# Modulation vectors of a two-layer trunk: formed by TensorE in four column groups, zero rows written by the fillers

## The chip, the core and the metric

One core of a Trainium2 chip runs the whole program in one launch. The metric is the device time of one execution in microseconds, the median of several. The engines of the core work in parallel, each through its own instruction queue in order: TensorE (matrix products, PE in the profile, its weight loads PEld), VectorE (DVE), ScalarE (ACT), GpSimd (POOL), and SyncE (SP), which issues most of the DMAs. Sixteen DMA engines carry the transfers. All tensors are float32.

## The reference

Two layers over 512 latent and 256 context tokens of 1024 channels. Each layer draws its modulation from two condition vectors:

```
s_lat, s_ctx = silu(c), silu(c_ctx)
sh1, sc1, g1, sh2, sc2, g2 = split(s_lat @ w_mod[layer] + b_mod[layer], 6)   # the same for s_ctx
h = rmsnorm(x, norm1_g) * (1 + sc1) + sh1
y = token_mixer(h)        # w_in, a short gated convolution beside RWKV-7 scans in both directions, gates, w_o
x = x + g1 * y
h2 = rmsnorm(x, norm2_g) * (1 + sc2) + sh2
x = x + g2 * hier_moe(h2) # the top expert group of 4, then the top 2 of its 8 SwiGLU experts
```

In the last layer the context feeds only the scans' first states. A final norm gives the output. The modulation is a product of two vectors of 1024 with a matrix of 1024 x 6144, per layer: 24 MB of weights that are read once.

## The kernel before

The 6144 modulation columns of a layer are worked off as twelve groups g of 512. Groups 0 and 1 are the shift sh1, 2 and 3 the scale sc1, 4 and 5 the gate g1, and so on. A group's weights are eight tiles of 128x512, one for each 128 inputs. The inputs, silu of both conditions, lie in `sc` (128 x 8 x 2).

The stages of a layer follow one another: a start-up (layer 0 only, `startup`), the dense stage (`stage_dense`, 15 products with w_in and what the scans need), the scans (`stage_scan`), the output products (`stage_out`), the 32 experts (`moe`, whose weights are 192 MB a layer), and `combine`. The scans are two passes of 12 chunks each, a chain of small products per chunk with copies by ScalarE and VectorE between them. Ahead of each six chunks `inverses` inverts triangular blocks by 31 steps of a multiply (line 834) and an add (line 836) on VectorE; TensorE takes them up at line 858.

Between the links of that chain TensorE is given other work, from a generator, `fillers` (line 638): the remaining products with w_in, the convolution, the gates, and w_a_out. It is advanced one `yield` at a time; a step is the products of one 128-channel tile of a filler (six in layer 0, three in layer 1). 12 and 18 steps are taken in the dense stage, the rest in the scans, 0.75 steps for each unit of weight that the chain's links state. TensorE's order is the written one in the dense stage and the scans (`manual_schedule`); that of VectorE, ScalarE, GpSimd and SyncE is the planner's, which may put an instruction well ahead of its place in the program once its inputs and buffers are there. In the start-up SyncE's order is the written one too.

The modulation vectors are made in two ways.

- Start-up, groups 0 to 3 of layer 0, `modulate` (line 251): two loads of 1 MB, eight products of the two columns of `sc` with 128x512 into one accumulator of two rows; ScalarE copies the two rows out (line 267), and four products turn them into columns (line 270).
- Everything else, 12 groups in the fillers of layer 0 (the last four are layer 1's) and 8 in those of layer 1, `mod_begin` and `mod_end` (lines 225 and 244), called by `more` (line 651) at 13 places of a layer's fillers. `mod_begin` loads eight tiles of 256 KB, ScalarE multiplies each by one column of `sc` for each condition that is needed (lines 237 and 240), and GpSimd adds it to an accumulator (line 241). The next `more` calls `mod_end`: four products with ones for each condition sum over the partitions (line 249), and `mod_store` adds the bias and derives what follows from it.

The experts' outputs go to `bufY` in HBM. Its part for overflowing experts, 24 x 64 rows (6.3 MB), is written with zeros in the start-up by `zero_rows` (line 160): three DMAs of 2 MB out of a tile of 128 zeros, in rows of 512 bytes.

PSUM buffers come by tag. `pd` has three, shared by the fillers' outputs (two in layer 0, one in layer 1), the final sums and, in the start-up, the accumulator.

Of the kernel before, what the change touches and what calls it, by code (L numbers as in the profile page):

```python
# [18 lines left out]
P = 128  # L19
D = 1024  # L20
KT = 8
# [46 lines left out]
for _n, _w in (("ident", 128), ("mask", 128), ("bones", 128), ("bmean", 128), ("ones", 128), ("ii", 64), ("tri", 128),  # L68
               ("i64", 64), ("i8", 8), ("i4", 4), ("i24", 24), ("i64k", 12), ("tok", 6)):
    CO[_n] = slice(_o, _o + _w)  # L70
    _o += _w
# [3 lines left out]
def constants():  # L75
    c = np.zeros((P, NCO), np.float32)
    p = np.arange(P)[:, None]
    q = np.arange(P)[None, :]
    c[:, CO["ident"]] = p == q
    s = p % C  # L80
    t = q % C
    c[:, CO["mask"]] = np.where(q < C, s < t, s <= t)
    c[:, CO["bones"]] = (p // 64) == (q // 64)
    c[:, CO["bmean"]] = ((p // 64) == (q // 64)) * (-1.0 / 64)
    c[:, CO["ones"]] = 1.0
    c[:, CO["ii"]] = (p % 64) == np.arange(64)[None, :]
    c[:, CO["tri"]] = p < q
    c[:, CO["i64"]] = np.arange(64)
    c[:, CO["tok"]] = p + P * np.arange(6)
    c[:, CO["i8"]] = np.arange(8)  # L90
    c[:, CO["i4"]] = np.arange(4)
    c[:, CO["i24"]] = np.arange(24)
    c[:, CO["i64k"]] = 64.0 * (1 + np.arange(12))
    m = np.zeros((P, T + 1024), np.float32)
    m[:, :T] = (np.arange(T) % C) != 0
    m[:, T:] = np.eye(32, dtype=np.float32).reshape(1, 1024)
    return c, m
# [16 lines left out]
class Trunk:  # L114
# [12 lines left out]
    def build(self):  # L127
        nc, tc, t = self.nc, self.tc, self.t
        with ExitStack() as es:
# [3 lines left out]
            sc = self.sc = self.sb(cp, [P, KT, 2], "sc")  # L133
# [11 lines left out]
            nc.vector.tensor_scalar(sc, th, 0.5, None, op0=ALU.mult)  # L145
# [14 lines left out]
    def zero_rows(self, pool):  # L160
# [6 lines left out]
        for i in range(0, n, 4096):  # L167
            nc.sync.dma_start(v[:, i:i + 4096].rearrange("p (a d) -> p a d", d=128),
                              rap(z[:], 0, [[0, 32], [1, 128]]))
# [55 lines left out]
    def mod_begin(self, l, g, pool, bufs):  # L225


        nc, t = self.nc, self.t
        ns = 2 if l == 0 or g < 4 else 1
        acc = [self.sb(pool, [P, 512], f"ma{s}") for s in range(ns)]  # L230
        for k in range(KT):
            w = self.sb(pool, [P, 512], "wm", bufs=bufs)
            nc.sync.dma_start(w, t["w_mod"][l, g][:, k, :])
            for s in reversed(range(ns)):
                c = self.sc[:, k, s:s + 1]
                if k == 0:
                    nc.scalar.activation(acc[s], w, AF.Copy, scale=c)  # L237
                else:
                    p = self.sb(pool, [P, 512], "wms") if s else w
                    nc.scalar.activation(p, w, AF.Copy, scale=c)  # L240
                    nc.gpsimd.tensor_tensor(acc[s], acc[s], p, op=ALU.add)  # L241
        return l, g, ns, acc

    def mod_end(self, l, g, ns, acc):

        ps = self.psum("pd", [P, 4, 2], bufs=3)
        for m in range(4):
            for s in range(ns):
                self.nc.tensor.matmul(ps[:, m, s:s + 1], acc[s][:, m * P:(m + 1) * P], self.k["ones"][:, :1],
                                      start=True, stop=True)  # L250
        self.mod_store(l, g, ns, ps)

    def modulate(self, l, g, pool, loads=()):

        nc, k = self.nc, self.k
        ps = self.psum("pd", [2, 512], 3)
        for h in range(2):
            w = self.sb(pool, [P, 4, 512], "wm", bufs=6)
            nc.sync.dma_start(w, self.t["w_mod"][l, g][:, 4 * h:4 * h + 4, :])
            for i in range(4):  # L260
                kt = 4 * h + i
                nc.tensor.matmul(ps, self.sc[:, kt, :], w[:, i, :], start=kt == 0, stop=kt == KT - 1)
            yield
        for src, dst in loads:
            nc.sync.dma_start(dst, src)
        row = self.sb(pool, [2, 512], "mrow", bufs=2)
        nc.scalar.activation(row, ps, AF.Copy)
        ps = self.psum("pc", [P, 4, 2], 2)
        for m in range(4):
            nc.tensor.matmul(ps[:, m, :], row[:, m * P:(m + 1) * P], k["ident"][:2, :2], start=True, stop=True)  # L270
        self.mod_store(l, g, 2, ps)
# [97 lines left out]
    def startup(self):  # L369

        nc, tc, k, V = self.nc, self.tc, self.k, self.nc.vector
        with tc.tile_pool(name="np", bufs=1, side=self.B, reuse_waits="tile") as np_:
# [20 lines left out]
            with tc.high_priority(offset=10000), tc.manual_schedule(engines=MAN(E)):  # L393
# [29 lines left out]
                self.zero_rows(np_)  # L423
# [215 lines left out]
    def fillers(self, fp, mods):  # L639
# [8 lines left out]
        mods = iter(mods)  # L648
        begun = []

        def more():
            if begun:
                self.mod_end(*begun.pop())
            g = next(mods, None)
            if g is not None:
                begun.append(self.mod_begin(*g, fp, 3))
        cw = pv[:, PV["cw"]].rearrange("p (w j) -> p w j", j=4)
        for j in range(4):
# [6 lines left out]
            groups = []  # L665
            for ps, s in (yield from self.w_in_parts(i0 + 1)):
# [16 lines left out]
        for m in range(16):  # L683
# [4 lines left out]
            if m % 2:  # L688
                more()
# [3 lines left out]
        for m in range(8):  # L693
            if m == 2:
# [858 lines left out]
```

## Time and profile before

| | |
|---|---|
| median of 3 runs | 3068.42 us (3065.1 to 3070.13) |
| profiled execution | 3077.6 us, its span 3075.6 us |
| PE | 2592.5 us (84%), 17281 instructions |
| PEld | 1718.6 us (56%) |
| DVE | 1332.2 us (43%), 2597 |
| ACT | 995.0 us (32%), 1839 |
| POOL | 716.2 us (23%), 778 |
| HBM | 647.41 MB read, 91.49 MB written, 240 GB/s over the span |
| mean granted TensorE clock | 0.909 of full speed |

Busy times are sums over the whole span; a share says how full an engine is, not whether anything waits for it. A float32 product stands in the trace as two records with a weight load each. The idle time given with an instruction is that of its engine just before it, and the name behind the arrow is what ended it. The granted clock is a mean over a stretch of the two levels, 1.2 and 2.4 GHz, in parts of the upper one.

### The profile page before, as it was taken

How to read it: one execution, taken by the hardware profiler on the slowest of the kernel's cores; microseconds unless marked ns; L12 is line 12 of the kernel's file. 1: busy time of each engine (PE TensorE's matmuls, PEld its weight loads, DVE VectorE, ACT ScalarE, POOL GpSimd, SP SyncE). 2: the span in 40 equal slices, each digit the busy share in tenths (PEclk: the TensorE clock that was granted, in tenths of full speed). 3: DMA queues.
4: the chain of work that ended last, by engine and by line, in shares of the span. 5: the costliest groups of instructions: out<-in, count | busy, mean ns of one | idle time of the engine just before them, and what ended most of it. 6: DMA issues, size and time to landing. Idle time of an engine off the chain costs nothing. (4 is left out here: it accounts for less than half of the span.)

```text
span 3075.6 us, 44626 instructions
## 1 busy us (share of the span) xinstructions
PE 2592.5 (84%) x17281; PEld 1718.6 (56%) x17281; DVE 1332.2 (43%) x2597; ACT 995.0 (32%) x1839; POOL 716.2 (23%) x778
## 2 busy tenths in 40 slices
PE   7998688798889699977887996788888969888886
PEld 4777576676778643333336775566666734333334
DVE  4786564656345421111115687556565431111113
ACT  4653445454512111111112553443442211111111
POOL 0431344544521100000002232233222021000001
PEclk9999898889889899999997998778899979999998
DMA  8456344443546699999994466444534599999994
GB/s 301 131 160 193 105 123 139 147 158 121 163 153 214 227 344 402 398 402 396 401 360 153 134 184 209 133 141 153 157 121 149 194 337 398 395 399 394 399 400 161
DMA packets 301974, 741.87 MB, mean 241 GB/s; under 512 B 55488, under 2 KB 140736, under 8 KB 250816
## 3 DMA queue, kind: packets, MB, share of 16 engines
q1 hardware_dynamic: 288480, 694.42, 62.7%
q0 software_dynamic: 13280, 44.57, 4.4%
q8 instruction: 137, 2.24, 0.3%
q14 instruction: 77, 0.63, 0.1%
HBM read 647.41 MB, written 91.49 MB: 240 GB/s over the span
## 5 line engine op out<-in xcount | busy, mean ns | idle before, releaser
L341 PE MATMUL pd<-hh,wh 128*128 128x512 f32 (+1 forms) x912 | 362.5, 437 | 11.1 <-DVE fo L1490 3.4
L341 PE MATMUL pd<-hh,wl 128*128 128x512 f32 (+1 forms) x912 | 318.9, 391 | 11.0 <-DVE wl L323 11.0
L341 PE MATMUL pd<-hl,wh 128*128 128x512 f32 (+1 forms) x912 | 318.4, 390 | 0.6 <-DVE hl L323 0.6
L323 DVE TENSOR_TENSOR wl<-wr,wh 128x512 fp32r<-128x512 f32 x236 | 183.5, 779 | 258.5 <-ACT wh L322 257.1
L1393 PE MATMUL pd<-ez,xs 128*64 128x512 f32 x1024 | 253.9, 630 | 39.3 <-DMA ez<-in_w 25.1
L1402 DVE COPY hs<-pd 128x512 f32<-128x512 f32 x65 | 45.0, 692 | 521.4 <-PE pd L1393 521.4
L322 ACT ACTIVATE wh<-wr 128x512 fp32r<-128x512 f32 x236 | 148.2, 629 | 295.7 <-PE pd L341 198.9
L241 POOL TENSOR_TENSOR ma<-ma,wm 128x512 f32<-128x512 f32 x140 | 187.2, 1337 | 164.5 <-ACT ma L237 118.2
L341 PEld LDWEIGHTS pd<-hh,wh 128*128 128x128 f32 x912 | 169.2, 204 | 59.2 <-issue 13.6
L1369 POOL DMA_INDIRECT xe<-h2rows,slot x64 | 60.0, 937 | 592.5 <-PE px L1381 552.8
L341 PEld LDWEIGHTS pd<-hh,wl 128*128 128x128 f32 x912 | 169.0, 204 | 48.8 <-DVE wl L323 15.0
L1414 DVE TENSOR_TENSOR yo<-py,yo 64x1024 f32<-64x1024 f32 x65 | 79.1, 1216 | 263.6 <-ACT yo L1413 252.3
L1406 PEld LDWEIGHTS pt<-cst,hs 128*128 128x128 f32 x1040 | 125.1, 191 | 112.7 <-issue 54.3
L341 PEld LDWEIGHTS pd<-hl,wh 128*128 128x128 f32 x912 | 170.3, 206 | 29.3 <-issue 1.9
L1393 PE MATMUL pd<-er,xs 128*64 128x512 f32 x672 | 169.4, 624 | 18.9 <-DMA er<-in_w 9.8
L1393 PEld LDWEIGHTS pd<-ez,xs 128*64 128x64 f32 x1024 | 78.0, 143 | 174.4 <-issue 126.6
L1406 PE MATMUL pt<-cst,hs 128*128 128x64 f32 x1040 | 141.3, 281 | 27.6 <-DVE hs L1402 17.4
L1393 PE MATMUL py<-ez,hid 128*64 128x512 f32 x520 | 123.3, 605 | 11.7 <-DVE yo L1414 7.4
L1415 POOL DMA_DIRECT2D bufY<-yo x65 | 35.5, 547 | 418.7 <-DVE yo L1414 391.7
L1408 ACT ACTIVATE hid<-pt 128x256 f32<-128x256 f32 x65 | 24.9, 383 | 321.4 <-PE pt L1406 320.7
L1383 ACT ACTIVATE xs<-px 128x512 f32<-128x512 f32 x65 | 38.8, 597 | 272.2 <-PE px L1381 263.1
L241 POOL TENSOR_TENSOR ma<-ma,wms 128x512 f32<-128x512 f32 x84 | 111.2, 1323 | 58.7 <-ACT wms L240 58.0
(379 smaller groups left out, 4977.8 us busy)
## 6 DMA issues: line engine op xcount, KB each, us to landing
ez<-in_w SPq DMA_DIRECT2D x193, 1024.0 KB, 22.6
er<-in_w SPq DMA_DIRECT2D x125, 1024.0 KB, 22.6
ex<-in_w SPq DMA_DIRECT2D x72, 1024.0 KB, 22.5
wr<-in_w_in SPq DMA_DIRECT2D x172, 256.0 KB, 3.1
wm<-in_w_mod SPq DMA_DIRECT2D x160, 256.0 KB, 3.5
bufY<-yo POOLq DMA_DIRECT2D x65, 256.0 KB
dKB<-KB SPq DMA_DIRECT2D x16, 768.0 KB, 4.5
dRR<-RR SPq DMA_DIRECT2D x16, 768.0 KB, 5.1
```

The source lines that it names most:

```text
L241: nc.gpsimd.tensor_tensor(acc[s], acc[s], p, op=ALU.add)
L322: self.nc.scalar.activation(hi, src, AF.Copy)
L323: self.nc.vector.tensor_tensor(lo, src, hi, op=ALU.subtract)
L341: nc.tensor.matmul(p, a[:, k], h[:, kt, s], start=kt == 0 and j == 0, stop=kt == nk - 1 and j == 2)
L1369: self.nc.gpsimd.indirect_dma_start(out=xe[:], out_offset=None, in_=self.h2[:], in_offset=bass.IndirectOffsetOnAxis(ap=slot, axis=0))
L1383: nc.scalar.activation(xs, ps, AF.Copy)
L1393: nc.tensor.matmul(out[h * CAP:(h + 1) * CAP, c:c + 512], a[:, kt, :], w[:, i + h, c:c + 512], start=kt < 2, stop=kt >= nk - 2)
L1402: nc.vector.tensor_copy(hs, ps)
L1406: nc.tensor.matmul(pt[:, i, c, :], hs[:, c * P:(c + 1) * P], k["ii"], start=True, stop=True)
L1408: nc.scalar.activation(hid, pt[:, 0], AF.Silu)
L1414: nc.vector.tensor_tensor(yo, py[:CAP], yo, op=ALU.add)
L1415: nc.gpsimd.dma_start(ydst, yo)
```

## The change

`sc` becomes 128 x 8 x 32, with zeros behind its two columns, so that a product with it fills 32 rows of PSUM. Product kt of a group goes to the rows from 32 x (kt mod 4): four column groups of the array, each with its own rows of one accumulator. ScalarE copies all 128 rows out; four products with a new constant `sel` (128 x 2, ones where the partition modulo 32 is 0 or 1) add the four column groups up and turn them into columns at once.

In the start-up two products fall on each column group and accumulate there. In the fillers a group comes in two halves of four tiles, one load of 1 MB each into a single buffer, four products that don't accumulate; the first half is copied to `row` by ScalarE, the second added to it by VectorE. `more` now does three things: the final sums of a finished group, the products of the half loaded at the call before, and the load of the next half. It is called twice as often. ScalarE's scalings and GpSimd's additions are gone; the products form both vectors for every group, of which the groups of layer 1 that need one store one.

`zero_rows` becomes a generator that writes 512 KB at a time, and in layer 0 each `more` advances it once: twelve DMAs from the fillers instead of three in the start-up.

```diff
-            sc = self.sc = self.sb(cp, [P, KT, 2], "sc")
+            sc = self.sc = self.sb(cp, [P, KT, 32], "sc")
...
+            nc.vector.memset(sc, 0.0)
+            nc.vector.tensor_scalar(sc[:, :, :2], th, 0.5, None, op0=ALU.mult)
...
+    c[:, CO["sel"]] = (p % 32) == np.arange(2)[None, :]
...
-        for i in range(0, n, 4096):
-            nc.sync.dma_start(v[:, i:i + 4096].rearrange("p (a d) -> p a d", d=128),
-                              rap(z[:], 0, [[0, 32], [1, 128]]))
+        for i in range(0, n, 1024):
+            nc.sync.dma_start(v[:, i:i + 1024].rearrange("p (a d) -> p a d", d=128),
+                              rap(z[:], 0, [[0, 8], [1, 128]]))
+            yield
...
-    def mod_begin(self, l, g, pool, bufs):
...
-    def mod_end(self, l, g, ns, acc):
...
+    def mod_load(self, l, g, h, n, pool, bufs):
+        w = self.sb(pool, [P, n, 512], "wm", bufs=bufs)
+        self.nc.sync.dma_start(w, self.t["w_mod"][l, g][:, h:h + n, :])
+        return w
+    def mod_products(self, ps, w, h, n):
+        for i in range(n):
+            kt = h + i
+            self.nc.tensor.matmul(ps[32 * (kt % 4):32 * (kt % 4) + 32, :], self.sc[:, kt, :], w[:, i, :],
+                                  start=kt < 4, stop=kt >= KT - 4)
+    def mod_rows(self, ps, pool, bufs):
+        row = self.sb(pool, [P, 512], "mrow", bufs=bufs)
+        self.nc.scalar.activation(row, ps, AF.Copy)
+        return row
+    def mod_sums(self, l, g, ns, row, tag, bufs):
+        ps = self.psum(tag, [P, 4, 2], bufs)
         for m in range(4):
+            self.nc.tensor.matmul(ps[:, m, :], row[:, m * P:(m + 1) * P], self.k["sel"], start=True, stop=True)
         self.mod_store(l, g, ns, ps)
     def modulate(self, l, g, pool, loads=()):
...
+        ps = self.psum("pd", bufs=3)
+        for h in (0, 4):
+            self.mod_products(ps, self.mod_load(l, g, h, 4, pool, 6), h, 4)
             yield
         for src, dst in loads:
+            self.nc.sync.dma_start(dst, src)
+        self.mod_sums(l, g, 2, self.mod_rows(ps, pool, 2), "pc", 2)
...
                 advance(self.modulate(0, 3, np_))
-                self.zero_rows(np_)
                 shifted(range(4, 8))
...
+        mods = ((i, h) for i in mods for h in (0, 4))
+        loaded, rows, done = [], [], []
+        zeros = self.zero_rows(fp) if l == 0 else iter(())
         def more():
+            if done:
+                i = done.pop()
+                self.mod_sums(*i, 2 if i[0] == 0 or i[1] < 4 else 1, rows.pop(), "pd", 3)
+            if loaded:
+                i, h, w = loaded.pop()
+                ps = self.psum("pd", bufs=3)
+                for kt in range(4):
+                    nc.tensor.matmul(ps[32 * kt:32 * kt + 32, :], self.sc[:, h + kt, :], w[:, kt, :],
+                                     start=True, stop=True)
+                if h:
+                    nc.vector.tensor_tensor(rows[0], rows[0], ps, op=ALU.add)
+                    done.append(i)
+                else:
+                    rows.append(self.mod_rows(ps, fp, 1))
+            i, h = next(mods, (None, 0))
+            if i is not None:
+                loaded.append((i, h, self.mod_load(*i, h, 4, fp, 1)))
+            next(zeros, None)
...
             groups = []
+            more()
...
+            more()
             for ps, s in (yield from self.w_in_parts(i0 + 2)):
...
-            if m % 2:
-                more()
+            more()
...
-            if m == 2:
+            if m in (2, 4):
                 more()
```

## Rows read from the trace of the kernel before

**Rows 1.** Windows by stage: length, busy time (instructions) by engine, granted clock, DMA share, GB/s

```profile
300.00:345.00 45.00, 20.83 (x188) 17.85 (x187) 38.00 (x61) 18.14 (x27) 20.88 (x16) 0.73 0.27 81
345.00:890.00 545.00, 473.79 (x4463) 389.55 (x4458) 289.23 (x617) 262.53 (x522) 246.60 (x253) 0.90 0.44 140
...
1090.00:1610.00 520.00, 447.15 (x2276) 190.73 (x2278) 80.37 (x116) 81.32 (x125) 43.38 (x60) 0.96 1.00 394
...
1940.00:2380.00 440.00, 376.19 (x3604) 284.37 (x3599) 241.93 (x541) 179.24 (x382) 129.15 (x170) 0.87 0.47 148
```

**Rows 2.** Costliest groups: GpSimd's additions (count, busy us, mean ns, idle before)

```profile
L241 POOL TENSOR_TENSOR ma<-ma,wm 128x512 f32<-128x512 f32 x140 | 187.2, 1337 | 164.5 <-ACT ma L237 118.2
...
L241 POOL TENSOR_TENSOR ma<-ma,wms 128x512 f32<-128x512 f32 x84 | 111.2, 1323 | 58.7 <-ACT wms L240 58.0
```

**Rows 3.** Timeline, first inverse of layer 0 (start, duration, operation, [idle before])

```profile
308.03 0.42 DVE L834 TENSOR_TENSOR tmp<-AlTc,Tl 128x252 f32<-128x252 f32 x1
...
314.49 1.38 DVE L834 TENSOR_TENSOR tmp<-AlTc,Tl 128x252 f32<-128x252 f32 x1
...
329.18 1.30 DVE L834 TENSOR_TENSOR tmp<-AlTc,Tl 128x192 f32<-128x192 f32 x1
...
338.93 1.49 PE L858 MATMUL pA<-AlTc,AM 32*32 32x32 f32 x48 [23.75 <-DVE AlTc L840]
```

**Rows 4.** Timeline, first inverse of layer 1

```profile
1905.01 1.37 DVE L834 TENSOR_TENSOR tmp<-AlTc,Tl 128x192 f32<-128x192 f32 x1
...
1917.21 1.36 DVE L836 TENSOR_TENSOR Tl<-Tl,tmp 128x252 f32<-128x252 f32 x1
...
1935.42 1.49 PE L858 MATMUL pA<-AlTc,AM 32*32 32x32 f32 x48 [27.08 <-DVE AlTc L840]
```

**Rows 5.** Timeline, a readout in the scan of layer 0

```profile
606.79 5.39 DVE L834 TENSOR_TENSOR tmp<-AlTc,Tl 128x252 f32<-128x252 f32 x1
...
615.04 1.20 PE L1004 MATMUL pA<-cst,yr 128*128 128x128 f32 x4 [9.07 <-DVE yr L312]
```

**Rows 6.** TensorE's groups in 340 to 890, the idle time before them

```profile
L952 PE MATMUL pc<-VU,KTr 128*64 128x64 f32 x352 | 17.4, 240 | 10.9 <-DVE VU L944 10.7
...
L1004 PE MATMUL pA<-cst,yr 128*128 128x128 f32 x44 | 9.1, 337 | 22.4 <-DVE yr L312 20.7 <-DVE AM L817 1.7
```

**Rows 7.** The same in 1940 to 2380

```profile
L943 PE MATMUL pc<-W,Rf 64*64 64x64 f32 x384 | 18.1, 240 | 23.0 <-ACT W L936 23.0
...
L1004 PE MATMUL pA<-cst,yr 128*128 128x128 f32 x32 | 7.1, 356 | 9.5 <-DVE yr L312 8.9 <-DVE AM L817 0.6
```

**Rows 8.** ScalarE's scalings in 1950 to 2370

```profile
L240 ACT ACTIVATE wm<-wm,sc 128x512 f32<-128x512 f32 x40 | 28.6, 719 | 41.2 <-DMA wm<-in_w_mod 40.1 <-POOL ma L241 0.8
```

**Rows 9.** Timeline of the start-up, TensorE, SyncE and ScalarE

```profile
6.80 8.47 PE L262 MATMUL pd<-wm,sc 128*2 128x512 f32 x16 [6.80 <-DMA wm<-in_w_mod]
...
23.80 22.23 SPq L168 DMA_DIRECT2D bufY<-zrow  x3
...
35.67 7.03 PE L262 MATMUL pd<-wm,sc 128*2 128x512 f32 x16
...
38.92 2.50 ACT L390 ACTIVATE nh<-xin,mod,am 128x512 f32<-128x512 f32 x4 [4.28 <-DVE mod L276]
...
61.32 0.50 PE L341 MATMUL pd<-hh,wh 128*128 128x512 f32 x1 [1.39 <-ACT hh L322]
```

**Rows 10.** Timeline of an expert: products that alternate between two column groups

```profile
1206.98 3.65 PE L1393 MATMUL pd<-ez,xs 128*64 128x512 f32 x16 [0.69 <-ACT xs L1383]
```

**Rows 11.** Timeline: final sums of two vectors and of one

```profile
310.11 1.84 PE L249 MATMUL pd<-cst,ma 128*128 128x1 f32 x16
...
1903.09 0.95 PE L249 MATMUL pd<-cst,ma 128*128 128x1 f32 x8
```

**Rows 12.** Timeline: the two pairs behind 64-row products

```profile
277.10 0.63 PE L341 MATMUL pd<-hh,wh 128*128 128x512 f32 x2
277.56 0.51 PE L341 MATMUL pd<-hl,wh 128*128 128x512 f32 x2
```

More of the change, by code (lines that the diff above doesn't have):

```diff
@@ L68 @@
 for _n, _w in (("ident", 128), ("mask", 128), ("bones", 128), ("bmean", 128), ("ones", 128), ("ii", 64), ("tri", 128),
-               ("i64", 64), ("i8", 8), ("i4", 4), ("i24", 24), ("i64k", 12), ("tok", 6)):
+               ("i64", 64), ("sel", 2), ("i8", 8), ("i4", 4), ("i24", 24), ("i64k", 12), ("tok", 6)):
     CO[_n] = slice(_o, _o + _w)
@@ L144, in build @@
             nc.vector.scalar_tensor_tensor(th, th, 1.0, cv, op0=ALU.add, op1=ALU.mult)
-            nc.vector.tensor_scalar(sc, th, 0.5, None, op0=ALU.mult)
+            nc.vector.memset(sc, 0.0)
+            nc.vector.tensor_scalar(sc[:, :, :2], th, 0.5, None, op0=ALU.mult)
             self.wp = es.enter_context(tc.tile_pool(name="wp", bufs=2, side="left", reuse_waits="tile"))
@@ L223, in weights @@
         return wh, wl
-    def mod_begin(self, l, g, pool, bufs):
[L228 to L242, printed above, removed]
@@ L244, in mod_end @@
-    def mod_end(self, l, g, ns, acc):
-        ps = self.psum("pd", [P, 4, 2], bufs=3)
+    def mod_load(self, l, g, h, n, pool, bufs):
[7 more added lines that the diff above has]
+                                  start=kt < 4, stop=kt >= KT - 4)
@@ L247, in mod_end @@
+    def mod_rows(self, ps, pool, bufs):
[4 more added lines that the diff above has]
+        ps = self.psum(tag, [P, 4, 2], bufs)
         for m in range(4):
-            for s in range(ns):
-                self.nc.tensor.matmul(ps[:, m, s:s + 1], acc[s][:, m * P:(m + 1) * P], self.k["ones"][:, :1],
-                                      start=True, stop=True)
+            self.nc.tensor.matmul(ps[:, m, :], row[:, m * P:(m + 1) * P], self.k["sel"], start=True, stop=True)
@@ L251, in mod_end @@
         self.mod_store(l, g, ns, ps)
     def modulate(self, l, g, pool, loads=()):
[L255 to L262, printed above, removed]
+        ps = self.psum("pd", bufs=3)
@@ L263, in modulate @@
+        for h in (0, 4):
+            self.mod_products(ps, self.mod_load(l, g, h, 4, pool, 6), h, 4)
             yield
         for src, dst in loads:
[L265 to L271, printed above, removed]
+            self.nc.sync.dma_start(dst, src)
@@ L647, in fillers @@
             nc.gpsimd.memset(z, 0.0)
-        mods = iter(mods)
-        begun = []
+        mods = ((i, h) for i in mods for h in (0, 4))
+        loaded, rows, done = [], [], []
+        zeros = self.zero_rows(fp) if l == 0 else iter(())
         def more():
[L652 to L656, printed above, removed]
+            if done:
[16 more added lines that the diff above has]
+            next(zeros, None)
         cw = pv[:, PV["cw"]].rearrange("p (w j) -> p w j", j=4)
```

## The prediction, made before the changed kernel ran

> **What bounds the kernel now.** I read the windows by stage first, then the timelines inside the scans, then TensorE's line table for its idle time.
>
> The windows [rows 1] split the span into kinds of stage. In the expert stage of either layer (1090 to 1610 stands for both) the DMA engines are full, at 394 GB/s. The change touches nothing there, so those 1040 us can only move as a block. In the scans (345 to 890 and 1940 to 2380) TensorE is busy 473.8 of 545 and 376.2 of 440 us and the DMA engines less than half: TensorE in its written order sets the pace, and its 71.2 and 63.8 idle us are what another engine can give back. Ahead of the scan of layer 0 (300 to 345) it is busy only 20.8 of 45 us, while VectorE works 38.0.
>
> The timeline of that place shows why. VectorE runs the triangular inverse, a chain of multiply and add; TensorE waits for it 23.75 us [rows 3]. The multiply of 128x252 takes 0.42 us at 308.03, and 1.38 at 314.49, when GpSimd has begun its additions. Eleven such operations, from 314.49 to 329.18, are stretched like that, about 0.94 us each. GpSimd's 140 + 84 additions are the modulation sums [rows 2], all of which the change removes. The inverse of layer 1 is caught too: seven operations from 1905.01 to 1917.21, 7.1 us too long in total, and 27.08 us of waiting TensorE behind them [rows 4]. Later the same thing hits the readouts: one multiply lasts 5.39 us at 606.79, and TensorE loses 9.07 us for a small norm queued behind it on VectorE [rows 5].
>
> **The change part by part.**
>
> *GpSimd's additions go.* The first inverses end the wait that TensorE stands in, so the stretch comes back whole: 11 x 0.94 = 10.4 us in layer 0 and 7.1 in layer 1. Two of the new VectorE additions (128x512 out of PSUM, an estimate of 0.7 us from the fillers' other operations of that size) may land in these chains: -17.5 + 1 = -16.5. What is late next there is the same chain at its unstretched speed, still over 10 us behind TensorE. In the rest of the scans TensorE's idle time by releaser [rows 6, 7] is 22.4 us for the norm and 10.9 for the solved update in layer 0, of which VectorE is the releaser almost everywhere; with two smaller groups some 42 us. Bounds: nothing comes back (the order of the queues makes them) or all 42 does; I take two thirds, 28, because the longest of them hold a stretched operation as in [rows 5]. In layer 1 the norm's 9.5 us and some 13 us of like waits: I take half, 11.
>
> *ScalarE's products go.* There is one beside each addition and one for each vector's first tile, 224 + 32 of 0.72 us, against 20 row copies. They stand in ScalarE's queue and wait there for their loads, 40.1 us in layer 1 [rows 8]; behind them stands the copy W, for which TensorE loses 23.0 us [rows 7]. Bounds 0 and 23 in layer 1, I take 9; 2 in layer 0, where that wait is smaller. Both scans together: 28 + 2 + 11 + 9 = -50.
>
> *TensorE gets the products.* 20 groups in the fillers, two halves each, four float32 products a half, each seen as two records: 40 x 8 records. One column group alone takes 7.03 us for 16 records [rows 9]. Two column groups alternating take 3.65 us for 16 [rows 10], so 1.8 for a half. The trace has no four groups: the ends are 1.8 us (no better than two) and 0.65 (perfectly parallel: two record lengths of 0.213 and a tail). I take 1.0, a little above half the price of two groups. About six of the 40 halves fall into the two waits for the first inverses and are free: 34 x 1.0 = +34. The final sums shrink: a group with both vectors took 16 records in 1.84 us, one with a single vector 8 in 0.95 [rows 11]; now all take 8. Eleven groups on the path save 0.87: -9.6. Switching between shapes costs some 0.12 us a side, as the pair after L815's 64-row products shows, 0.63 against 0.51 [rows 12]: 34 x 2 x 0.1 = +7. The new accumulators share the three buffers of pd with the fillers' outputs; the copy that frees one stands mostly a whole product behind. Nothing to 0.8 us a half; I take +3.
>
> On those shapes the Trainium skill says in "TensorEngine Tiling (Array Packing)", Key Properties, that changing the tiling mode drains the engine. It names no price; [rows 12] show 0.12. "TensorE: Matmul & The Clock Gate", Measured speedup vs the span model, gives 2.38 times for three column tiles at N=512. By it, as an estimate, a half would cost 7.03 / 2 / 2.38 = 1.5 us instead of 1.0, and the sum would be 17 us higher, near 3042.
>
> *The startup.* Four vector groups of 7.03 us stand in TensorE's order [rows 9], and the dense stage begins after the fourth, held by ScalarE's shifted inputs: the first half of them starts at 38.92, the second only when the fourth group's sums are there, and TensorE's last wait for them ends at 61.32. With 16 records in some 2 us instead of 7.03, the first spread need not queue behind the products (2.6 us earlier), its scale is done by 31 to 32, and ScalarE's two halves run back to back: about 16.2 us of shifting and splitting from 32, with 2 us of row copies and weight splits, end near 50 instead of 62. That is 12 us; if the first sums queue behind VectorE as now, 35.5 + 18 gives 8. The final sums get 0.8 us longer each, hidden beside ScalarE. I take -11, ends -5 and -14.
>
> *The zero rows.* Three issues hold SyncE's queue 22.23 us from 23.80 [rows 9], but the loads of the first three weight tiles are ahead of them, and TensorE waits for ScalarE, not for weights, so taking them from there gives nothing by itself. The twelve smaller ones carry the same 6.3 MB. Their order on SyncE is free: the planner may put them at the fillers' places or, as nothing holds them but the memory of their zero tile, together behind the startup, 12 x 1.85 us of issue ahead of weight loads. Spread, they cost nothing beside a DMA share of 0.44 [rows 1]. Bunched they can cost up to 10 us. I take +2.
>
> *Dense stage of layer 0.* A first group of sums that was planned into it no longer stretches VectorE: -1.
>
> Sum: -16.5 - 50 + 34 - 9.6 + 7 + 3 - 11 + 2 - 1 = -42.1 us. Against the profiled execution's 3077.6 us (span 3075.6 and 2.0 around it) that is 3035.5. This execution is 9.2 us above the median of the runs shown, 3068.42, so the forecast is 3026 us.
>
> **The rivals.**
>
> *The stalls are the order's, not GpSimd's* (chance 0.12). Then only inverses and startup come back. For it: each copy W has to follow TensorE's own products, whoever else uses ScalarE. Against: the stretched operations lie right inside the longest. -42 + 50 = +8, less some 10 that the shorter queues give anyway: 3066, no change.
>
> *Four groups run like two* (0.13): 34 x 0.8 = +27 and 3 more in the startup: 3056. For it: two groups are all the trace shows. Against: each of the two reaches the full rate.
>
> *Slower: TensorE waits for the halves* (0.10). The products stand in TensorE's written order, and the single buffer lets the next half's 1 MB be asked for only after the last products. For the first such load of the startup TensorE waited until 6.80 us [rows 9]. Eight filler steps are about 8.4 us of TensorE in layer 0 and some 5 in layer 1, stretched by the scan's own work to 10 to 20. If the issue stands behind a weight load that itself waits for a buffer, the half comes late, and the whole scan stops behind it, where until now only ScalarE and GpSimd did. It decides from 42 / 40 = 1.05 us a half; at 3 us it is +120: 3146.
>
> *More comes back* (0.08): all of the 42 and 23 us and a clock that stays at its upper level more than now (0.90 and 0.87 in the scans): 2980.
>
> **How the numbers follow.** The forecast's mechanism has 0.57, with its own range of 2995 to 3050. The range of 2984 to 3068 takes in the two rivals near no change and leaves out the slower one and most of the largest gain. 0.2% is about what a measurement of this kernel tells from no change (6 us). Faster by more: 0.57 + 0.08 + 0.13 and a little of the first rival, 0.80. Slower: 0.10 and a tail of the others, 0.12. Within: 0.08.
>
> **What would show it.** Right: no GpSimd additions; the multiplies of 128x252 in the first inverses at 0.42 us, TensorE's waits there near 14 and 20 us; idle time ahead of L1004 in layer 0 under 10 us; a half's 8 records in about 1 us; the first dense product's last wait near 50 us; expert stages at the same length. Wrong: TensorE waiting for the load of a half; halves of 1.8 us or more; weight loads late behind bunched zero rows at 50 to 70 us; the same idle time with VectorE unstretched.

## The result and the profile after

The changed kernel takes 2962.7 us (median of four, 2958.5 to 2971.3) where the kernel before took 3069.3 beside it: a ratio of 0.965, 95% interval 0.961 to 0.969. The forecast was 3026, a gain of 42 us; it is 106, and below the lower end of the range. The profiled execution (2971.3 us, span 2969.3) stands 106.3 us below the one of before, so its stages carry the whole difference.

The stages are cut at the same events in both kernels: first product of the scan's operands, TensorE's take-up of the first inverse, its first product with W, its last product of a readout norm. The windows (columns as in [rows 1]) of the kernel after, from the start to the end of the first scan and then from the second layer's operands to the end of its scan:

```profile
0.00:268.25 268.25, 226.31 (x1148) 170.67 (x1149) 174.44 (x289) 126.78 (x225) 55.36 (x55) 0.96 0.62 195
268.25:329.82 61.57, 50.73 (x343) 40.09 (x343) 45.42 (x101) 17.22 (x41) 3.89 (x4) 0.92 0.60 204
329.82:360.43 30.61, 30.61 (x342) 24.38 (x342) 6.63 (x10) 12.62 (x29) 0.32 (x1) 0.72 0.42 130
360.43:826.90 466.47, 438.15 (x4278) 346.50 (x4278) 235.18 (x621) 152.48 (x348) 65.37 (x112) 0.96 0.49 154
...
1791.98:1863.02 71.04, 42.20 (x245) 30.34 (x244) 43.30 (x99) 16.52 (x39) 5.73 (x10) 0.81 0.64 214
1863.02:1883.66 20.64, 20.55 (x284) 14.44 (x284) 4.65 (x7) 10.34 (x22) 0.32 (x1) 0.76 0.48 149
1883.66:2255.96 372.30, 340.02 (x3406) 250.21 (x3406) 215.22 (x522) 141.02 (x318) 66.44 (x112) 0.94 0.50 155
```

Cut at the same events, the scans of the kernel before and the stage between them read:

```profile
363.99:892.54 528.55, 457.73 (x4230) 376.39 (x4230) 285.62 (x614) 252.01 (x497) 246.28 (x252) 0.89 0.44 140
892.54:1864.23 971.69, 836.35 (x4448) 508.01 (x4446) 348.97 (x637) 244.83 (x405) 161.23 (x174) 0.93 0.79 295
1957.55:2361.76 404.21, 346.72 (x3334) 262.03 (x3334) 230.99 (x519) 168.33 (x359) 120.01 (x154) 0.88 0.47 148
```

Against the forecast, stage by stage (us; the stages of before that are not shown lasted 266.46, 72.47 and 25.06, then 71.19 and 22.13 in layer 1):

| stage | forecast | measured |
|---|---|---|
| start to the first operands (startup -11, zero rows +2) | -9 | +1.8 |
| first inverses, both layers, with the stretch behind each | -16.5 | -10.9 + 5.6 - 0.2 - 1.5 = -7.0 |
| scans: idle time -50; products, sums, switches, buffers +34.4 | -15.6 | -62.1 - 31.9 = -94.0 |
| everything else | -1 | -7.1 |

So the gain and the error both lie in the scans. There TensorE's idle time (length less busy time) went from 70.8 to 28.3 us and from 57.5 to 32.3: -67.7. But its busy time, which should have risen by 34, fell by 26.3, and the granted clock beside it rose from 0.89 and 0.88 to 0.96 and 0.94. The fillers' products show it best, since the scan of layer 0 has the same 322 records of each form in both kernels. In the groups by line, before:

```profile
L341 PE MATMUL pd<-hh,wh 128*128 128x512 f32 x322 | 107.9, 417 | 3.1 <-ACT cvo L686 2.7 <-DVE uv L669 0.4
L341 PE MATMUL pd<-hl,wh 128*128 128x512 f32 x322 | 92.0, 370 | 0.0
```

and after, with the new products, the sums, and the groups that answer to [rows 6]:

```profile
L331 PE MATMUL pd<-hh,wh 128*128 128x512 f32 x322 | 100.0, 391 | 0.8 <-DVE mod L266 0.6
L331 PE MATMUL pd<-hl,wh 128*128 128x512 f32 x322 | 85.8, 349 | 0.0
...
L651 PE MATMUL pd<-wm,sc 128*32 128x512 f32 x144 | 19.6, 615 | 1.8 <-ACT cvo L693 1.4 <-DVE mod L266 0.3
L250 PE MATMUL pd<-cst,mrow 128*128 128x2 f32 x80 | 9.8, 245 | 0.0
...
L958 PE MATMUL pc<-VU,KTr 128*64 128x64 f32 x352 | 15.6, 229 | 0.6 <-DVE VU L950 0.5
...
L1010 PE MATMUL pA<-cst,yr 128*128 128x128 f32 x48 | 8.3, 295 | 6.6 <-DVE yr L302 5.9 <-DVE AM L823 0.7
```

The eighteen halves of this scan cost 19.6 us, 1.09 each, and the sums 9.8 where the old ones took 20.8. All other records of TensorE together took 408.8 us instead of 436.9: 28.1 us at a better clock, a term that the sum did not have. Idle time ahead of the norm is 6.6 us for 22.4, ahead of the solved update 0.6 for 10.9. In the second scan, after (compare [rows 7]):

```profile
L949 PE MATMUL pc<-W,Rf 64*64 64x64 f32 x384 | 16.4, 224 | 4.5 <-ACT W L942 4.5
...
L1010 PE MATMUL pA<-cst,yr 128*128 128x128 f32 x32 | 6.4, 330 | 10.0 <-DVE yr L302 9.5 <-DVE AM L823 0.6
```

The first inverses, in the timeline after (the rows answer to [rows 3, 4]; the last row is layer 1):

```profile
309.83 0.42 DVE L840 TENSOR_TENSOR tmp<-AlTc,Tl 128x252 f32<-128x252 f32 x1
...
329.82 1.49 PE L864 MATMUL pA<-AlTc,AM 32*32 32x32 f32 x48 [10.72 <-DVE AlTc L846]
...
1863.02 1.49 PE L864 MATMUL pA<-AlTc,AM 32*32 32x32 f32 x48 [17.40 <-DVE AlTc L846]
```

The operations run unstretched, and the waits are 13.0 and 9.7 us shorter. In layer 0 the stage up to the take-up is 10.9 us shorter. The stretch behind it then takes 30.61 us, all of it busy, at a clock of 0.72, where before it took 25.06 at 0.89. That is this execution's clock rather than a price of the change: in three of the runs below that only write the zero rows elsewhere (startup, gates by VectorE, gates by ScalarE) the same stretch takes 24.9 to 25.2 us at 0.91 to 0.92. The last of the three:

```profile
322.35:347.48 25.13, 25.13 (x343) 20.23 (x343) 6.63 (x10) 12.55 (x29) 0.32 (x1) 0.92 0.48 158
```

In layer 1 the stage keeps its length, 71.0 us for 71.2. VectorE's 31 steps begin 36.3 us after the first product of the operands instead of 32.9, and end, with the other work between them, after 34.7 us more instead of 38.2. The products and sums of the modulation fill 6.1 us of TensorE's time here instead of 0.9, which shortens its wait without shortening the stage. The loads of the operands are waited for about as long as before, 8.9 us in all for 8.0. The longest of these waits before, then after:

```profile
1873.96 1.97 PE L815 MATMUL pA<-RRi,KBi 64*128 64x64 f32 x16 [4.11 <-DMA RRi<-dRR]
...
1882.71 1.97 PE L815 MATMUL pA<-RRi,KBi 64*128 64x64 f32 x16 [3.92 <-DMA RRi<-dRR]
```

```profile
1803.82 1.97 PE L821 MATMUL pA<-RRi,KBi 64*128 64x64 f32 x16 [5.04 <-DMA RRi<-dRR]
...
1811.58 1.98 PE L821 MATMUL pA<-RRi,KBi 64*128 64x64 f32 x16 [3.14 <-DMA RRi<-dRR]
```

The startup after, in the timelines of TensorE and SyncE (compare [rows 9]):

```profile
6.81 1.93 PE L238 MATMUL pd<-wm,sc 128*32 128x512 f32 x8 [6.81 <-DMA wm<-in_w_mod]
...
35.86 1.92 PE L238 MATMUL pd<-wm,sc 128*32 128x512 f32 x16
...
54.99 0.50 PE L331 MATMUL pd<-hl,wh 128*128 128x512 f32 x1 [0.38 <-DVE hl L313]
...
57.42 10.79 SPq L170 DMA_DIRECT2D bufY<-zrow  x7
69.88 7.70 SPq L170 DMA_DIRECT2D bufY<-zrow  x5
...
84.54 0.80 PE L331 MATMUL pd<-hh,wh 128*128 128x512 f32 x1 [3.14 <-ACT wh L312]
```

Sixteen records take 1.92 us instead of 7.03, and the last wait for ScalarE's and VectorE's split inputs ends at 54.99. Before, it was the one behind the record that [rows 9] ends with:

```profile
62.31 0.50 PE L341 MATMUL pd<-hl,wh 128*128 128x512 f32 x1 [0.38 <-DVE hl L323]
```

So it ends 7.3 us earlier. Then the twelve zero DMAs go out in two bunches, and at 84.54 TensorE waits 3.14 us for a weight tile that came late; the windows of that place show the clock falling with it, and 10 us later at 0.77:

```profile
80.00:90.00 10.00, 6.86 (x19) 4.09 (x19) 3.31 (x5) 4.90 (x9) 0.00 (x0) 0.72 0.58 183
90.00:100.00 10.00, 10.00 (x35) 6.77 (x35) 3.80 (x4) 4.90 (x10) 2.15 (x1) 0.77 0.06 19
```

### The profile page after: what moved, and what is told of

It reads as the page before. It is cut to its first block, busy times and chain, and to the rows that moved or that the text cites. A ratio compares the mean times of both kernels' runs of the same rounds, so it can differ in the third digit from the quotient of the medians.

```text
span 2969.3 us, 44287 instructions
## 1 busy us (share of the span) xinstructions
PE 2571.9 (87%) x17505; PEld 1677.7 (57%) x17505; DVE 1237.5 (42%) x2618; ACT 838.4 (28%) x1603; POOL 422.9 (14%) x554
## 5 line engine op out<-in xcount | busy, mean ns | idle before, releaser
L331 PE MATMUL pd<-hh,wh 128*128 128x512 f32 (+1 forms) x912 | 352.4, 426 | 11.7 <-ACT hh L312 3.8
L331 PE MATMUL pd<-hh,wl 128*128 128x512 f32 (+1 forms) x912 | 311.7, 382 | 10.3 <-DVE wl L313 10.3
L331 PE MATMUL pd<-hl,wh 128*128 128x512 f32 (+1 forms) x912 | 311.7, 382 | 1.1 <-DVE hl L313 1.1
L1399 PE MATMUL pd<-ez,xs 128*64 128x512 f32 x1024 | 257.4, 635 | 37.6 <-DMA ez<-in_w 27.0
L313 DVE TENSOR_TENSOR wl<-wr,wh 128x512 fp32r<-128x512 f32 x236 | 166.2, 705 | 245.0 <-ACT wh L312 244.0
L331 PEld LDWEIGHTS pd<-hl,wh 128*128 128x128 f32 x912 | 164.5, 198 | 29.5 <-DVE hl L313 2.3
L1399 PE MATMUL pd<-ex,xs 128*64 128x512 f32 x384 | 99.9, 644 | 21.7 <-DMA ex<-in_w 16.7
L1399 PEld LDWEIGHTS pd<-er,xs 128*64 128x64 f32 x672 | 48.9, 143 | 112.9 <-issue 83.6
L1410 ACT ACTIVATE hs<-pd 128x512 f32<-128x512 f32 x65 | 38.8, 597 | 240.9 <-PE pd L1399 240.8
```

Source lines behind the costliest of these rows:

```text
L313: self.nc.vector.tensor_tensor(lo, src, hi, op=ALU.subtract)
L331: nc.tensor.matmul(p, a[:, k], h[:, kt, s], start=kt == 0 and j == 0, stop=kt == nk - 1 and j == 2)
L1399: nc.tensor.matmul(out[h * CAP:(h + 1) * CAP, c:c + 512], a[:, kt, :], w[:, i + h, c:c + 512], start=kt < 2, stop=kt >= nk - 2)
L1410: nc.scalar.activation(hs, ps, AF.Copy)
```

## The experiments

To compare kernels I use the sum of the six stages around the scans (operands to take-up, take-up to first W, scan, in both layers): 1123.6 us before, 1022.6 after. Each comes from one profiled execution. In three runs below that have the same products in the scans and only write the zero rows elsewhere (startup, spread, gates by ScalarE) it reads 1017 to 1029, so differences of that size say nothing. Ratios are to the kernel before, timed in the same session, with 95% intervals.

**GpSimd's adds put back.** To the changed kernel:

```
+    w = loaded[-1][2]                       # the half just asked for
+    for kt in range(4):
+        for s in range(ns):
+            if h + kt: nc.gpsimd.tensor_tensor(dum, w[:, kt, :], w[:, (kt + 1) % 4, :], op=ALU.add)
```

> The changed kernel with GpSimd's 224 additions put back as idle ballast: behind each load of a half as many 128x512 additions of two SBUF tiles as before, into a scratch tile that nobody reads. ScalarE's scalings stay out, TensorE's products stay. Theory A (the additions stretch VectorE's operations with two SBUF inputs, TensorE waits, and its granted clock falls with the waiting): most of the gain of the two scans goes again, 3030 to 3060 us against 2963, clock of the scans back at 0.88 to 0.91, TensorE's idle time in them up by 50 us or more. Theory B (ScalarE's scalings held the chain): at most 20 us more, 2965 to 2985. Theory C (the new products or the new order of the queues lift the clock by themselves): 2963 to 2975, clock stays at 0.94 to 0.96.

Measured 3042.0 us, ratio 0.991 (0.988 to 0.994): 79 us over the changed kernel, stages 1094. The time is the one that theory A asked for. The clock and the idle time are not: the scans read 0.92 and 0.93, and TensorE's idle time in them is 62.4 and 37.6 us, 39 more than in the changed kernel. VectorE is busy 288.6 us in the first scan again, 235.2 in the changed kernel. The multiplies of the inverses, in the groups by line of that scan, here and in the changed kernel:

```profile
L846 DVE TENSOR_TENSOR tmp<-AlTc,Tl 128x31 f32<-128x31 f32 (+15 forms) x93 | 48.8, 525 | 1.4
```

```profile
L840 DVE TENSOR_TENSOR tmp<-AlTc,Tl 128x31 f32<-128x31 f32 (+15 forms) x93 | 34.4, 370 | 1.4
```

**ScalarE's scalings put back** (`nc.scalar.activation(dum, w[:, kt, :], AF.Copy, scale=self.sc[:, h + kt, s:s + 1])` in the same loop, every `kt`).

> The changed kernel with ScalarE's 256 scalings of 128x512 put back as ballast, into a scratch tile that nobody reads; no additions. Theory A: a little, from ScalarE's queue alone, 2970 to 2990. Theory B: 3030 to 3060. Theory C: 2963 to 2975.

Measured 3025.8 us, 0.986 (0.983 to 0.988): 63 us over the changed kernel, stages 1085, VectorE unstretched (235.5). That lies between theory A, which had it 7 to 27 us over the changed kernel, and theory B. ScalarE in its first scan stands still for the loads of these tiles:

```profile
L665 ACT ACTIVATE dum<-wm,sc 128x512 bf16<-128x512 f32 x136 | 97.8, 719 | 37.0 <-DMA wm<-in_w_mod 34.6
```

**GpSimd occupied without reading**: two memsets of 0.63 us in place of each add of 1.33 us. One small ScalarE instruction for each half, a copy of two columns of it, binds the memsets to the load.

> The changed kernel with GpSimd kept about as long as by the additions, but by memsets that read nothing (two of 640 columns for each addition, bound to the load of the half). Theory A, because VectorE is held by GpSimd's reads: 2960 to 2975. If GpSimd's occupation delays its own part of the chain (the scaling of the state and of RR): as with the additions, 3030 to 3060. Theory C: 2963 to 2975 too.

Measured 2982.5 us, 0.972 (0.969 to 0.975), 20 us over the changed kernel and 7 past the range of theory A; stages 1033, 11 over it. GpSimd is as busy as with the adds (217.0 us for 226.9 in the first scan), VectorE's multiplies are at 368 ns. What stretches VectorE is that the adds read, not that GpSimd works:

```profile
L848 DVE TENSOR_TENSOR tmp<-AlTc,Tl 128x31 f32<-128x31 f32 (+15 forms) x93 | 34.2, 368 | 1.4
```

The Trainium skill states this in "SBUF — State Buffer", Who interferes with whom: a VectorE instruction with two SBUF inputs contends with a GpSimd instruction that reads SBUF, not with one that only writes it. The two runs, 525 against 368 ns, agree.

What the 20 us are is open. One candidate is ScalarE: at the small instruction it waits for the loads, in the first scan 41.4 us, longer than at the scalings of the run before:

```profile
L663 ACT ACTIVATE dum<-wm 128x2 bf16<-128x2 f32 x17 | 3.5, 203 | 42.4 <-DMA wm<-in_w_mod 41.4 <-POOL S L936 1.0
```

That scan is only 5.0 us longer than in the changed kernel for it (471.5 for 466.5).

**Adds and scalings put back together**, each scaling in place by one, so that the products read the same data.

> The changed kernel with both: ScalarE scales every half in place by one (so it still waits for each load), and GpSimd's 224 adds of two tiles follow it. If adds and scalings explain the whole result, the two must give back the 106 us and the products' own time on TensorE besides (40 x 1.1 us in the scans less the old sums of 20 us): 3080 to 3110. Rival: the new products and the order of records that goes with them lift the clock by themselves: 3030 to 3060.

Measured 3164.0 us, 1.031 (1.026 to 1.036): 201 us over the changed kernel, stages 1210, more than both alone (72 + 62) and past the kernel before. It is past both ranges of the expectation. It was no copy of the old form (its products now wait for the scalings, and TensorE's idle time in the first scan is 96.3 us, 70.8 in the kernel before), so it gives no price for the old form and does not decide whether the new products gain by themselves. The runs that follow bear on that.

**The kernel before without the adds, and without adds and scalings.** `nc.gpsimd.tensor_tensor(acc[s], acc[s], p, op=ALU.add)` taken out; then the two activations as well, with the loads and sums left. Both form other modulation vectors.

> The kernel before without GpSimd's 224 adds (the sum over the eight tiles is left out, so the modulation vectors are wrong; loads, scalings and final products stay). The adds alone: if they are most of what the change took away, 3005 to 3020, idle time of TensorE in the first scan from 71 down to 45 us. Rival: the scalings' waits for loads hold TensorE as long without them: 3040 to 3060.

> The kernel before with neither adds nor scalings (each vector's final products read the first loaded tile; products over the eight tiles are left out). The loads stay. This is the floor without any modulation work beside the scan: if the products of the change cost what their records show (34 halves of 1.1 us, 37 us on TensorE, less the final sums' 10 us), 2930 to 2945. Rival: the new order of records and products lifts the clock by itself, then the floor lies no lower than the changed kernel: 2960 to 2975.

In total 3067.9 us, 0.998 (0.996 to 1.001), and 3078.9, 1.002 (1.000 to 1.004): by the total no gain at all. The windows show why the total misleads. First scan, the stage between the scans, second scan, without the adds:

```profile
365.44:871.35 505.91, 460.74 (x4230) 379.17 (x4230) 229.37 (x614) 235.97 (x471) 64.56 (x112) 0.89 0.45 140
871.35:1868.30 996.95, 858.99 (x4518) 514.77 (x4517) 346.75 (x640) 255.09 (x421) 153.56 (x169) 0.93 0.81 298
1956.15:2350.10 393.95, 347.85 (x3334) 263.47 (x3334) 211.89 (x519) 160.68 (x347) 65.91 (x112) 0.88 0.47 143
```

and with neither:

```profile
360.39:815.74 455.35, 428.62 (x4230) 353.69 (x4230) 228.63 (x614) 146.86 (x339) 64.67 (x112) 0.96 0.40 124
815.74:1891.73 1075.99, 883.10 (x4663) 525.17 (x4662) 351.06 (x646) 246.33 (x407) 155.21 (x173) 0.91 0.80 297
1974.17:2347.00 372.83, 338.15 (x3334) 255.83 (x3334) 213.80 (x519) 138.06 (x313) 65.73 (x112) 0.91 0.44 134
```

The middle stage, which holds the first experts, lasts 25 and 104 us longer with 70 and 215 more records of TensorE than before: other vectors send other tokens to the experts. The scans have the same records (4230 and 3334) as before and can be compared. The stages around them are 1083.2 and 995.4 us. So by these traces taking the adds away gives 40 us, the scalings another 88, and the new products cost 27 on top of that floor (1022.6 - 995.4).

The last two numbers are loose. The profiled execution with neither, 3060.0 us, is the fastest of its ten and 18.9 below their median; those of before and after lie 8 and 9 above theirs. No trace says in which stages the other executions are longer, so the 88 can be too large by up to 27 us and the 27 can be nothing. Less the growth of the middle stage, the median is 2974.6 us (3078.9 - 104.3), in the rival's range, and the profiled execution 2955.7, in neither. So the price of the new products stays open. Not open is the rival's reason: the first scan reaches a clock of 0.96 without the new products, so it does not take them to lift it.

What I expected of the adds alone, most of the result, is wrong. TensorE's idle time in the first scan fell from 70.8 to 45.2 us, as that theory asked, but its busy time did not fall (457.7 and 460.7). With the adds gone ScalarE waits more, 93.7 us for loads in the first scan, where it waited 14.5 for loads and 27.4 for GpSimd:

```profile
L240 ACT ACTIVATE wms<-wm,sc 128x512 f32<-128x512 f32 x56 | 40.5, 723 | 93.9 <-DMA wm<-in_w_mod 93.7
```

and the clock of the first scan stays at 0.89. When the scalings go too, another 18.5 us of idle time and 32.1 of busy time go with them.

TensorE's idle time in the scans, summed by the engine that ended it (us):

| ended by | before | without the adds | with neither | after |
|---|---|---|---|---|
| VectorE, first scan | 41.9 | 15.1 | 12.3 | 12.6 |
| ScalarE, first scan | 28.5 | 29.5 | 14.0 | 15.1 |
| VectorE, second scan | 17.5 | 12.2 | 17.5 | 15.2 |
| ScalarE, second scan | 39.0 | 32.8 | 15.9 | 15.6 |

In the first scan each engine's part goes with its own work: VectorE's with the adds, half of ScalarE's with the scalings. The two largest waits for ScalarE in the first scan before (total, times, longest):

```profile
PE py L966 <- ACT KTr L901: 9.0, 8, 3.3
PE pc L943 <- ACT W L936: 7.2, 4, 3.3
```

**How the scalings cost.** Three runs of the changed kernel with them: reading the constants' tile; reading the half whose products run in the same call; reading the tile that ScalarE itself has just written (`more(cg)` and `more(tg)` hand it over).

> The run with ScalarE's 256 scalings again, but they read the constants' tile and not the half on its way, so that ScalarE never waits for a load (34.6 us of DMA wait in the first scan there). If that wait, with the copies of W, of the vectors and of the readout queued behind it, is what the scalings cost: 2965 to 2985. Rival: it is ScalarE's time itself (0.72 us each in front of those copies): 3010 to 3030.

2981.7 us, 0.970 (0.966 to 0.975). It tells nothing of the scans: with no input from there to hold them, the scalings were moved out: into the startup (ScalarE is busy 216.7 us there, 126.8 without them), the stage behind it (51.0 for 17.2) and the stage between the scans (280.0 for 239.9). Its 19 us over the changed kernel are spread; no stage holds more than 7.4 of them.

> The changed kernel with ScalarE's 256 scalings in the scans, of the half whose products run in the same call, loaded one call before: ScalarE has them to do in the same stretches but should find the half landed. In the last try with a resident tile the scalings left the scans altogether (ScalarE is as busy in the first scan as in the changed kernel, 152 us), so it told nothing of their time. Waits for loads as the cost: 2970 to 2990. ScalarE's time in front of the copies as the cost: 3010 to 3030.

3032.5 us, 0.987 (0.984 to 0.990), stages 1083. Not cheaper, and still 45.9 us of waits for the halves in the first scan: a load that is asked for one call earlier has not landed when ScalarE comes to it.

> The changed kernel with ScalarE's scalings again, each reading the tile that ScalarE itself has just written (the gates' tanh or the convolution's copy), so that none waits for a load and none can leave its place. Waits for loads as the cost: 2965 to 2985, TensorE's idle time in the first scan near 30 us. ScalarE's own time (0.72 us a scaling in front of the copies) as the cost: 3015 to 3035, idle time 45 to 50 us.

2986.9 us, 0.973 (0.970 to 0.976), stages 1047.5, first scan 487.1 us for 497.7 in the run with load waits. In that scan 130 scalings, for 136 with the waits, now wait 2.8 us in all:

```profile
L664 ACT ACTIVATE dum<-cvo,sc 128x512 bf16<-128x512 f32 x96 | 69.1, 720 | 2.1
...
L664 ACT ACTIVATE dum<-cg,sc 128x512 bf16<-128x512 f32 x34 | 24.5, 720 | 0.7
```

So 39 of the 63 us go when the scalings no longer wait for loads (3025.8 - 2986.9), and 24 stay, with the scalings' own time in front of the copies that TensorE needs. That is nearer to the theory of the waits, 2 us past its range. But the waits by themselves are not worth 39: the run with the memsets has 41.4 us of them in its first scan and stands 20 us over the changed kernel in all. The two add up to less apart (24 and at most 20) than together.

**One column group for four** (`ps[:32, :]` for `ps[32 * kt:32 * kt + 32, :]`, accumulating over `kt`; copy, add and sums on 32 rows).

> The changed kernel, but the fillers' products go through one column group (32 columns, eight records one behind the other) and the copy, the add and the sums take 32 rows. A half then has 8 records of about 0.38 us (the 128x512 products of L331), 3.0 us for 1.1. If TensorE's time sets the scans: 40 x 1.9 = 76 us longer, some of it given back by a clock that falls less: 3015 to 3040. Rival: the 28 and 32 us in which TensorE still stands idle in the scans take up much of it: 2985 to 3005.

Measured 3044.2 us, 0.990 (0.986 to 0.993): 81 us over the changed kernel, 4 past the range. A half takes 3.62 us where four groups take 1.06:

```profile
621.26 3.62 PE L651 MATMUL pd<-wm,sc 128*32 128x512 f32 x8
```

```profile
611.53 1.06 PE L651 MATMUL pd<-wm,sc 128*32 128x512 f32 x8
```

Forty halves are by that 102 us longer, and 81 show: in these stages TensorE's own time is the bound, and only a fifth is hidden. Four groups run 3.4 times as fast as one. "TensorE: Matmul & The Clock Gate", Measured speedup vs the span model, in the Trainium skill, has 2.38 times for three column tiles and no row for four.

**The zero rows**, four places. In the startup as before (three DMAs); spread from the first call of the fillers on, each bound to its place by a tile that VectorE makes as zero times the half just loaded; the same in the gates' loop only; there, but from a tile that ScalarE makes out of the gate tile it has just written:

```
-        nc.gpsimd.memset(z, 0.0)                        # once, ahead of the loop
+            z = self.sb(pool, [P, 128], "zrow", bufs=1)   # for each DMA
+            nc.scalar.activation(z, self.zsrc, AF.Copy, scale=0.0)
```

> The changed kernel with the zero rows written as before, three DMAs of 2 MB in the start-up behind the last modulation load. If the twelve small ones, which the planner put in two bunches at 57 to 78 us, cost the dense stage its 3.1 us wait for a weight tile and the low clock behind it (81 to 95 us): 5 to 10 us less, 2953 to 2958. If they cost nothing: 2963; if the three large ones hold the first weights instead: 2968 to 2975.

> The changed kernel, but each of the twelve zero DMAs reads a tile that VectorE makes as zero times the half just loaded, so that it can't go out before its place in the scan. If the two bunches of zero DMAs at 57 and 70 us are what took the startup's gain (they hold the DMA engines ahead of the weights, TensorE then waits 3.1 us at 84.5 and runs at the lower clock until 95): start to first projection 268 -> 258 to 262 us, in all 2953 to 2960. Rival: the first weights are late for another reason, as in the run with the zero DMAs in the startup, where TensorE waited 9.5 us for them: 2960 to 2968.

> The zero rows' twelve DMAs one in each of twelve calls in the gates' loop, later than in the run that spread them from the first call on, where start to first projection fell from 268 to 260 us but the stage behind it grew from 62 to 69 (they lie beside the loads of the first inverses' operands). If that is the cause, both gains stay: 2950 to 2957. Rival: the stage behind the startup waits for its operands whatever lies beside them: 2960 to 2968.

> The zero rows' DMAs in twelve calls of the gates' loop, each from a tile that ScalarE makes as zero times the gate tile it has just written, so that no engine waits for a load. If VectorE's waits for loads took the startup's gain back in the scan: 2945 to 2956. Rival: twelve DMAs of 512 KB beside the scan cost it that much wherever their zeros come from (its DMA share is 0.52 against 0.47): 2960 to 2975.

| | total (us) | ratio | start to operands | to take-up | scan 0 |
|---|---|---|---|---|---|
| after | 2962.7 | 0.965 (0.961 to 0.969) | 268.3 | 61.6 | 466.5 |
| startup | 2969.9 | 0.968 (0.966 to 0.971) | 266.0 | 62.1 | 467.7 |
| spread | 2961.5 | 0.964 (0.960 to 0.968) | 260.2 | 69.4 | 467.8 |
| gates, VectorE | 2975.7 | 0.967 (0.963 to 0.971) | 260.1 | 61.7 | 481.5 |
| gates, ScalarE | 2953.7 | 0.962 (0.959 to 0.965) | 260.4 | 62.0 | 471.1 |

With the DMAs out of the startup, the time to the first operands is 8 us shorter than after and 6 shorter than before. Spread from the first call on, the next stage takes that back. In the gates' loop VectorE's twelve multiplies stood in its queue waiting for loads, the scan took it back (15 us), and the total is past both ranges:

```profile
L169 DVE TENSOR_SCALAR zrow<-wm 128x128 f32<-128x128 f32 x12 | 2.7, 222 | 37.1 <-DMA wm<-in_w_mod 33.8 <-issue 3.3
```

Without that wait most is kept: 2953.7 us, the fastest kernel here. Its interval still overlaps that of the changed kernel, so the 9 us rest on the stages as much as on the totals. Its window at the place shown above:

```profile
80.00:90.00 10.00, 10.00 (x46) 6.92 (x46) 5.82 (x6) 6.94 (x13) 2.20 (x1) 1.00 0.08 28
```

## Why the prediction was wrong, step by step

*The sign, the bound and the products were right.* TensorE in the scans is the bound (the run with one group shows it), GpSimd's reads stretch VectorE, a half costs 1.09 us for a forecast of 1.0, the multiplies are at 0.42 us, and TensorE does not wait for the halves, so the slower rival fell; "four groups run like two" fell too. The sums fell by 11.0 us in layer 0's scan (20.8 to 9.8) and 1.1 in layer 1's, 12.1 for a forecast of 9.6. The adds' part of the first scan's idle time was sized well, too: without them the idle time that VectorE ends fell by 26.8 us, for 28.

*"ScalarE's products go", 9 + 2 us, is the step that failed first.* I priced it by one copy, W, for which TensorE waited 7.2 us in the first scan and 23.0 in the second. Over all its copies ScalarE ended 28.5 and 39.0 us of TensorE's idle time, and 13.4 and 23.4 of that went: 36.8 us where I had 11. The part that VectorE ends fell by 29.3 and 2.3, 31.6 where I had 28 and 11. So the adds, which I took for most of the gain, give 40 us by themselves, and it took the scalings' going to bring the rest. Put back behind the new products, the scalings alone cost 63 us. Why they cost that much is in part open, as the runs above say.

*The clock stood at zero in the sum, and that is the larger error.* Rows that I had shown read 0.90 and 0.87 [rows 1]. In the changed kernel they read 0.96 and 0.94, and the same records of TensorE took 28.1 us less in the first scan and 17.1 in the second (346.7 less 8.8 for the old sums is 337.9; 340.0 less 11.5 and 7.7 for products and new sums is 320.8). That is 45 of the 78 us by which the scans were missed; the idle time has 18 of it, and 15 come from the term for products, sums, switches and buffers: 28 halves fell into the scans, not 34, and with the sums they cost 19.0 us net, not 34.4. I had the mechanism only as a clause of the rival "more comes back", at 2980 us; that rival came nearest, and was still 17 us short.

*"I take two thirds", idle time -50*: it is -67.7. The norm's wait in layer 0 fell by 15.8 and the solved update's by 10.3 of 10.9; in layer 1 the norm's stayed (9.5 to 10.0) and the wait for W fell from 23.0 to 4.5, which I had put at 9.

*The first inverses.* In layer 0 "comes back whole" was right: the stage is 10.9 us shorter for 10.4 worked out. The 5.6 us that the stretch behind it lost are the low clock of this one execution; I had no price for it, and three other runs do not show it. In layer 1 it was wrong: nothing of the 7.1 us is kept, and in the four runs that only write the zero rows elsewhere at most 3 (68.2 to 71.5 us for 71.2). The kernel before without the adds shows that it could be: there VectorE's steps begin at 32.7 us, last 31.2, and the stage is 64.0 us for 71.2. With the new products they begin 3.6 us later and last 3.5 longer. The loads of the operands are not the reason: in those four runs, with the same halves beside them, they are waited for 6.4 to 7.6 us, less than the 8.0 before. Which part of the new work takes the time back was not tested.

*The startup, -11, and the zero rows, +2.* The last wait ended 7.3 us earlier, where I took 11 with ends of 5 and 14 (the 61.32 of [rows 9] was the last wait but one), and the bunching that I priced at up to 10 us happened and cost 8: start to operands +1.8 after, -6.1 with the zero DMAs in the gates' loop. With them in the startup nothing is gained either: there TensorE waits 9.5 us for weights whose loads are issued behind them, from 44.8 us on. "Taking them from there gives nothing by itself" held only as long as ScalarE was later than the weights.

What stays open is what the clock follows. It is not the idle time alone: the first scan had 45.2 us idle at 0.89 without the adds, 62.4 at 0.92 with the adds behind the new products, and 34.5 at 0.92 with the scalings that read what is there.

## What to carry to other kernels

When an engine's work is to go, price it by all the idle time of the bounding engine that it ends, not by the largest single wait, and take the sum from a kernel without that work (a floor), in several executions. Give the bounding engine's clock a term of its own whenever idle time goes: here it was larger than the error in the idle time. An instruction that waits for a load is a risk in the queue of an engine that the bound waits for (twelve on VectorE cost the scan 15 us), and a transfer that is to go late must read something that exists only late. Where an experiment changes data that steers the work, compare stages with equal record counts, not totals.

## What the runs showed of the chip that I had not expected

- Four column groups of 32 for eight records of 128x512 float32: 1.06 us a half, one group 3.62 us, 3.4 times.
- GpSimd memsets of 0.63 us left VectorE's multiplies at 368 ns; adds that read two tiles put them at 525 ns.
- The first scan's clock was 0.89 with the adds gone and 0.96 with the scalings gone too, with the same 4230 records of TensorE, whose busy time fell from 460.7 to 428.6 us; 460.7 x 0.89 / 0.96 is 427.
